# One kernel, one change: the recurrence's triangular inverse loads its operands at once, stores on GpSimd's queue, and its second half is issued behind the first half's recurrence

## The chip, the cores and the metric

The kernel runs on one core of a Trainium2 chip, in float32 with split products (each operand as a high and a low part, three matmuls per product). The metric is the device time in microseconds (us) of one execution. Engine names are those of the profile: PE (TensorE), DVE (VectorE), ACT (ScalarE), POOL (GpSimd), SP (SyncE, which issues nearly all DMAs).

## The reference, cut to what matters

Two blocks run one after the other on x of 1024 rows by 1024 columns. In the first, a projection feeds three mixers (an RWKV7 recurrence with 8 heads, a sparse attention with 4 heads, an attention to a memory), and their outputs, side by side, go through an out projection and a norm. The second block (a second mixer and a mixture of experts) is not touched by the change.

```python
def rwkv7_scan(r, decay, k, v, kk, a):
    def step(S, inp):
        r_t, w_t, k_t, v_t, kk_t, a_t = inp
        sa = einsum('bhvk,bhk->bhv', S, -kk_t)
        S = S * w_t + sa[..., None] * (kk_t * a_t) + v_t[..., None] * k_t
        return S, einsum('bhvk,bhk->bhv', S, r_t)
...
y = concat([rwkv7_group(...), nsa_group(...), memory_attention(...)])   # 512 + 256 + 256 columns
x = rms_norm(x + y @ w_out, norm_final_g)
```

The kernel does the recurrence in chunks. Inside a chunk the steps depend on each other through a lower triangular matrix, whose inverse is needed before the chunk's products.

## The kernel before

The first block's rows are cut into two halves of 512 rows, each of four tiles of 128 rows. A half goes through these steps, each a Python generator that issues instructions and yields a cost:

- `first_stage` and `att_proj`: the input projections. PE's products are pcm (L272); each weight piece is loaded (wraw, L229), copied by ACT to its high part (whi, L232) and subtracted by DVE to its low part (wlo, L233).
- `recur(H)`: first `inverse(H)`, then `rwkv_tile` for four tiles (masked products E on DVE, L757; pXk, L771; pX, L799), then the last tile's end.
- `attend(H)`: memory attention (`mem_tile`) and sparse attention (`nsa_tile`) for each tile. Both end in `finish_heads`, which norms the heads (DVE, with a power on POOL, L189), transposes them (PE's pfin, L898) and stores them to d_y.
- `third_stage(H)`: `close_first` with the out projection (`out_proj`), which reads d_y back (yr, L1147, with its parts yh and yl), multiplies (PE's pout, L1171), adds to the rows (DVE's rr, L1174) and norms them; then the second mixer. The out projection takes the column groups in the order 2, 3, 0, 1: group 2 is the sparse attention's, group 3 the memory attention's.

`inverse(H)` does, for the 64 blocks of 32x32 of each of two heads' halves at once: four times a load of two operands (AB, on SP's queue), a product (pN, L696), a mask (N on DVE, L698) and four stores of 32 KB to DRAM (d_n, L701); then one load of all of d_n into another layout (NTt, L704), and a forward substitution of 31 steps on DVE, each a product (scr, L712) and an addition (Ti, L714), one behind the other: 62 instructions, here called the chain. ACT makes a transposed copy (Tt, L716), and two stores (d_t) hand the result to `rwkv_tile`, which loads it as D and TT.

All four AB tiles use one buffer (tag "BK"), so that each load waits for the product before it.

What runs beside what is set by `weave`: each stream has a start time and a rate, the stream with the lowest time issues next, and each yielded cost times the rate moves it on. A scheduler then moves instructions within each engine's row, and each engine executes its row in order. There are three weaves. The second holds the projections, `recur(0)` and `attend(0)`; the third holds `third_stage(0)`, `recur(1)` and `attend(1)`, until the last two are through; the rest of `third_stage(0)` follows.

Of the kernel before, what the change touches and what calls it, by code (L numbers as in the profile page):

```python
# [25 lines left out]
CS = 64  # L26
# [74 lines left out]
def body(tc, a, out, stop=None, dbg=None):  # L101
    nc = tc.nc
# [89 lines left out]
    H2 = T // 2  # L192
# [16 lines left out]
    def R1(name):  # L209
        return ps_tile("r", name)  # L210
# [462 lines left out]
    d_n = dram.tile([2, 4, 8, 4, 32, 32], F32, name="d_n")  # L673
    d_t = dram.tile([2, 2, 4, 8, 4, 32, 32], F32, name="d_t")
# [6 lines left out]
    def rtile(tag, shape, bufs=1, name=None):  # L681
        return rw.tile([P] + shape, F32, tag=tag, name=name or tag, bufs=bufs)

    def inverse(H):

        ts = slice(TH * H, TH * H + TH)
        for p in range(4):
            AB = rtile("BK", [2, H2], name="AB")
            nc.sync.dma_start(ch(AB[:, 0]), d_AR[8 * H:8 * H + 8, :, p, 0].rearrange("c q t -> q c t"))
            nc.sync.dma_start(by_tile(AB[:, 1]), d_BK[ts, :, p, 0].rearrange("n q t -> q n t"))  # L690
            yield 0.6
            ps = R1("pN")
            for c in range(8):
                sl = slice(c * CS, (c + 1) * CS)
                for r in lohi:
                    nc.tensor.matmul(ps[r, sl], AB[r, 1, sl], AB[r, 0, sl], start=True, stop=True)  # L696
            N = rtile("UV", [8, CS], name="N")
            nc.vector.tensor_tensor(N, ch(ps), emask[:, None, 0:64].to_broadcast([P, 8, 64]), op=OP.mult)  # L698
            for q in range(4):
                b = (q % 2) * 32  # L700
                nc.sync.dma_start(d_n[H, q, :, p].rearrange("c s t -> s c t"), N[q * 32:q * 32 + 32, :, b:b + 32])  # L701
            yield 0.401
        NTt = rtile("X0", [32, 32], name="NTt")
        nc.sync.dma_start(NTt.rearrange("p s t -> p (s t)"), d_n[H].rearrange("q c p s t -> (q c p) (s t)"))  # L704
        Ti = rtile("GT", [32, 32], name="Ti")
        nc.gpsimd.memset(Ti, 0.0)
        nc.gpsimd.memset(Ti.rearrange("p a b -> p (a b)")[:, 0:1024:33], 1.0)
        scr = rtile("scr", [256])
        for s in range(31):
            nt, nj = 31 - s, s + 1  # L710
            sv = scr[:, :nt * nj].rearrange("p (t j) -> p t j", j=nj)
            nc.vector.tensor_tensor(sv, NTt[:, s, s + 1:32, None].to_broadcast([P, nt, nj]),  # L712
                                    Ti[:, s, None, 0:nj].to_broadcast([P, nt, nj]), op=OP.mult)
            nc.vector.tensor_tensor(Ti[:, s + 1:32, 0:nj], Ti[:, s + 1:32, 0:nj], sv, op=OP.add)  # L714
        Tt = rtile("X0", [32, 32], name="Tt")
        nc.scalar.activation(Tt, Ti.rearrange("p t j -> p j t"), AF.Copy)  # L716
        for x, src in ((0, Ti), (1, Tt)):
            nc.sync.dma_start(d_t[H, x].rearrange("q c p s t -> (q c p) (s t)"), src.rearrange("p a b -> p (a b)"))
        yield 0.979

    state = [None]
# [367 lines left out]
        yield 0.097  # L1089

    def recur(H):
        yield from inverse(H)
        for i in range(TH * H, TH * H + TH):
            yield from rwkv_tile(i)
        yield from ends.pop()

    def attend(H):
        for i in range(TH * H, TH * H + TH):
            yield from mem_tile(i)
            yield from nsa_tile(i)  # L1100
# [496 lines left out]
    def weave(*streams, until=()):  # L1597


        live = [[t0, n, g, rate] for n, (g, t0, rate) in enumerate(streams)]  # L1600
        wait = set(until) or set(range(len(streams)))
        while wait:
            s = min(live, key=lambda z: z[:2])
            c = next(s[2], None)
            if c is None:
                live.remove(s)
                wait.discard(s[1])
            else:
                s[0] += c * s[3]
# [11 lines left out]
    def narrow(g, J, V):  # L1621
        ring.update(J=J, V=V)
        yield from g

    def third_stage(H):
        with ExitStack() as st:
            rows = yield from close_first(H, pool("wkD", 1, stack=st))
            h2 = turn_rows(rows)
        yield 6
        yield from second_mixer(H, h2)  # L1630

    weave((first_stage(0), 0, 1))
    ring.update(J=["pj", "s"])
    weave((chain(att_proj(0), mem_kv(), first_stage(1), att_proj(1)), 0, 1),
          (recur(0), 0, 3.135),
          (narrow(attend(0), ["pj"], ["v"]), 90.8, 1.849))
    s1.close()
    g0 = third_stage(0)
    weave((g0, 0, 1), (recur(1), 9.9, 1.618), (attend(1), 0.1, 0.554), until=(1, 2))
    if "y" in dbg:  # L1640
        nc.sync.dma_start(dbg["y"], d_y)
    s2.close()
# [281 lines left out]
    with tc.manual_schedule(engines={mybir.EngineType.PE, mybir.EngineType.DVE, mybir.EngineType.Pool}):  # L1924
# [6 lines left out]
        with tc.For_i(0, n_ov, 1) as j:  # L1931
# [13 lines left out]
            b = NPAIR % 2  # L1945
# [68 lines left out]
```

## Time and profile before

| | |
|---|---|
| time, median of 3 runs | 2520.39 us (2517.54 to 2523.12) |
| the profiled execution | 2521.22 us, of which 2519.4 us are its span |
| PE busy | 2386.9 us, 95% of the span |
| DVE busy | 1543.9 us, 61% |
| ACT busy | 754.7 us, 30% |
| POOL busy | 349.6 us, 14% |
| granted TensorE clock, mean | 0.978 |

The span runs from the first to the last instruction of the execution. The granted clock is a share of full speed: 1.00 is the level of 2.4 GHz, 0.50 that of 1.2 GHz, and a value between is a window that held both. A matmul at 0.50 stays busy twice as long, so a window's time lost for PE is its length less busy time times clock.

### The profile page before, as it was taken

The page shows a single profiled execution, that of the slowest core. Times are in us where ns is not written, and L with a number is a line of the kernel's source. Part 1 is how long each engine was busy: PE and PEld are TensorE (multiplying, and loading weights), DVE is VectorE, ACT ScalarE, POOL GpSimd, SP SyncE. Part 2 cuts the span into 40 slices and gives each one's busy share as a digit, 9 for nine tenths or more (in the row PEclk, how much of TensorE's full clock was granted, in tenths as well). Part 3 has the DMA queues.
Part 4 walks back from the last instruction along what each step waited for, and adds up shares of the span by engine and source line. Part 5 has one row for each costly group of instructions (what it writes and reads, how often), then busy time and mean ns, then how long its engine had stood idle before and what let it go on. Part 6 is the DMA issues. An engine that isn't in the chain of part 4 may idle for free. (4 is left out here: it accounts for less than half of the span.)

```text
span 2519.4 us, 36225 instructions
## 1 busy us (share of the span) xinstructions
PE 2386.9 (95%) x13656; PEld 1545.4 (61%) x13656; DVE 1543.9 (61%) x3112; ACT 754.7 (30%) x1488; POOL 349.6 (14%) x472
## 2 busy tenths in 40 slices
PE   8989999999979999999999969999999999999997
PEld 6766777777757777787888824444444444444443
DVE  5537666754877676666665655555555555555555
ACT  4423554433445443343242411111111111111112
POOL 3000000010001011101120011111111111111112
PEclk9989999999979999999999979999999999999999
DMA  7667545544533222545355678999999999999991
GB/s 172 163 146 194 154 109 133 130 114 130 162 93 88 72 79 61 156 142 158 104 176 170 244 284 364 411 409 413 408 408 413 410 408 413 407 410 409 413 408 79
DMA packets 354176, 605.65 MB, mean 240 GB/s; under 512 B 124584, under 2 KB 299056, under 8 KB 329424
## 3 DMA queue, kind: packets, MB, share of 16 engines
q1 hardware_dynamic: 346592, 594.49, 65.6%
q0 software_dynamic: 5168, 8.69, 1.0%
q8 instruction: 109, 1.79, 0.3%
q14 instruction: 67, 0.55, 0.1%
q10 hardware_dynamic: 2240, 0.14, 0.1%
HBM read 563.46 MB, written 48.30 MB: 243 GB/s over the span
## 5 line engine op out<-in xcount | busy, mean ns | idle before, releaser
L1740 PE MATMUL pgu<-mw,xT 128*64 128x512 f32 x2048 | 461.4, 598 | 2.3 <-DVE up L1745 2.3
L272 PE MATMUL pcm<-hTh,whi 128*128 128x512 f32 (+1 forms) x912 | 369.2, 405 | 0.2 <-ACT whi L232 0.2
L272 PE MATMUL pcm<-hTh,wlo 128*128 128x512 f32 (+1 forms) x912 | 363.4, 398 | 0.5 <-DVE wlo L233 0.5
L272 PE MATMUL pcm<-hTl,whi 128*128 128x512 f32 (+1 forms) x912 | 363.6, 399 | 0.0
L233 DVE TENSOR_TENSOR wlo<-wraw,whi 128x512 fp32r<-128x512 f32 (+1 forms) x300 | 209.4, 702 | 185.9 <-ACT whi L232 160.7
L232 ACT ACTIVATE whi<-wraw 128x512 fp32r<-128x512 f32 (+1 forms) x300 | 187.0, 626 | 442.0 <-PE pcm L272 314.3
L1740 PEld LDWEIGHTS pgu<-mw,xT 128*64 128x64 f32 x2048 | 142.8, 137 | 265.9 <-issue 255.0
L1798 DVE TENSOR_TENSOR mw<-psp,mw 128x1024 f32<-128x1024 f32 x248 | 292.5, 1220 | 8.8 <-PE psp L1790 5.1
L1790 PE MATMUL psp<-yo,wt 128*128 128x512 f32 x1024 | 274.9, 410 | 4.1 <-DVE mw L1798 3.2
L1790 PEld LDWEIGHTS psp<-yo,wt 128*128 128x128 f32 x1024 | 182.7, 188 | 139.0 <-issue 80.6
L1768 PE MATMUL pyd<-mw,hT 128*64 128x512 f32 x1008 | 229.9, 598 | 2.3 <-DVEq L1931 2.3
L1744 DVE SCALAR_TENSOR_TENSOR mth<-mth,pgu 64x512 f32<-64x512 f32 x64 | 43.5, 679 | 290.5 <-ACT mth L1743 290.4
L272 PEld LDWEIGHTS pcm<-hTh,wlo 128*128 128x128 f32 (+1 forms) x912 | 170.7, 187 | 40.7 <-issue 3.8
L272 PEld LDWEIGHTS pcm<-hTh,whi 128*128 128x128 f32 (+1 forms) x912 | 170.8, 187 | 39.1 <-issue 5.4
L272 PEld LDWEIGHTS pcm<-hTl,whi 128*128 128x128 f32 (+1 forms) x912 | 171.0, 187 | 35.4 <-issue 2.9
L1743 ACT ACTIVATE mth<-pgu,rq 64x512 f32<-64x512 f32 x64 | 43.8, 684 | 493.4 <-PE pgu L1740 493.4
L1775 ACT ACTIVATE yo<-pyd,gt 64x512 fp32r<-64x512 f32 x128 | 87.6, 685 | 305.6 <-PE pyd L1768 304.3
L1777 DVE SCALAR_TENSOR_TENSOR yo<-pyd,gt,yo 64x512 fp32r<-64x512 f32 x128 | 96.0, 750 | 126.3 <-ACT yo L1775 125.3
L1783 POOL TENSOR_SCALAR wt<-rcon,tfs 128x128 fp32r<-128x128 f32 x256 | 150.4, 607 | 148.4 <-PE psp L1790 127.5
L1768 PEld LDWEIGHTS pyd<-mw,hT 128*64 128x64 f32 x1008 | 66.9, 136 | 126.7 <-issue 123.2
L1802 POOL DMA_INDIRECT xg<-d_x,idxt x32 | 34.4, 1076 | 690.0 <-issue 630.9
L1171 PE MATMUL pout<-whi,yh 128*128 128x512 f32 x256 | 107.4, 421 | 5.2 <-DVE rr L1174 5.1
(480 smaller groups left out, 3431.7 us busy)
## 6 DMA issues: line engine op xcount, KB each, us to landing
mw<-in_w_gate_dram SPq DMA_DIRECT2D x64, 2048.0 KB, 13.8
mw<-in_w_up_dram SPq DMA_DIRECT2D x64, 2048.0 KB, 9.5
mw<-in_w_down_dram SPq DMA_DIRECT2D x63, 2048.0 KB, 13.8
wraw<-in_w_in_dram SPq DMA_DIRECT2D x216, 256.0 KB, 3.1
wraw<-in_w_out_dram SPq DMA_DIRECT2D x32, 256.0 KB, 2.6
yr<-d_y SPq DMA_DIRECT2D x32, 256.0 KB, 3.1
d_x<-rr SPq DMA_DIRECT2D x16, 512.0 KB, 3.0
wraw<-in_w_o_dram SPq DMA_DIRECT2D x32, 256.0 KB, 3.0
```

The source lines that it names most:

```text
L232: nc.scalar.activation(hi, raw, AF.Copy)
L233: nc.vector.tensor_sub(lo, raw, hi.bitcast(F32))
L272: nc.tensor.matmul(ps[0:n], w, h[:, k], start=(k == 0 and j == 0), stop=(k == KD - 1 and j == 2))
L1171: nc.tensor.matmul(ps, y[:, t], w, start=(k == 0 and j == 0), stop=(k == 1 and j == 2))
L1740: nc.tensor.matmul(ph_[lohi[s]], xT[:, k], pieces[s][:, k * 512:(k + 1) * 512], start=(k == 0), stop=(k == KD - 1))
L1743: nc.scalar.activation(th, ph_[0:64], AF.Tanh, scale=rq[:, 0, h:h + 1])
L1768: nc.tensor.matmul(py[s][lohi[s]], hT[:, k, lohi[h]], piece[:, k * 1024 + s * 512:k * 1024 + s * 512 + 512], start=(k == 0), stop=(k == 3))
L1775: nc.scalar.activation(y[:, 0, 512 * s:512 * s + 512], py[s][o], AF.Copy, scale=gt[o, h:h + 1])
L1777: nc.vector.scalar_tensor_tensor(y[:, 1, 512 * s:512 * s + 512], py[s][o], gt[o, h:h + 1], y[:, 0, 512 * s:512 * s + 512].bitcast(F32), op ...
L1783: nc.gpsimd.tensor_scalar(w[0:n, i], iota[0:n], sh[0:n, i:i + 1], None, op0=OP.is_equal)
L1790: nc.tensor.matmul(ps[:, cs], w[0:n], yo[0:n, x, cs], start=(start and x == 0), stop=(x == 1))
L1798: nc.vector.tensor_tensor(x2, ps, x2, op=OP.add)
```

## The change

1. All eight loads of AB are issued together, into four buffers (three in a tile of tag "E", one of tag "BK"); the four N tiles get buffers of their own (tags "UV" and "GT").
2. The 16 d_n stores, the NTt load and the two d_t stores of each half are issued on GpSimd's queue, no longer on SP's.
3. `inverse(1)` is issued at the end of `recur(0)`, in the second weave, no longer at the start of `recur(1)`, in the third.
4. Rates: `attend(0)` in the second weave 1.849 to 1.76. In the third weave `recur(1)` starts at 0.2 with rate 1.9 (before 9.9 and 1.618), and `attend(1)` has rate 0.8 (before 0.554).

```diff
@@ -684,24 +684,26 @@
     def inverse(H):
 
         ts = slice(TH * H, TH * H + TH)
-        for p in range(4):
-            AB = rtile("BK", [2, H2], name="AB")
+        e_, b_ = rtile("E", [3, 2, H2], name="AB"), rtile("BK", [2, H2], name="AB")
+        ABs = [e_[:, 0], e_[:, 1], e_[:, 2], b_]
+        Ns = [t[:, p] for t in (rtile("UV", [2, 8, CS], name="N"), rtile("GT", [2, 8, CS], name="N")) for p in range(2)]
+        for p, AB in enumerate(ABs):
             nc.sync.dma_start(ch(AB[:, 0]), d_AR[8 * H:8 * H + 8, :, p, 0].rearrange("c q t -> q c t"))
             nc.sync.dma_start(by_tile(AB[:, 1]), d_BK[ts, :, p, 0].rearrange("n q t -> q n t"))
-            yield 0.6
+        yield 0.6
+        for p, (AB, N) in enumerate(zip(ABs, Ns)):
             ps = R1("pN")
             for c in range(8):
                 sl = slice(c * CS, (c + 1) * CS)
                 for r in lohi:
                     nc.tensor.matmul(ps[r, sl], AB[r, 1, sl], AB[r, 0, sl], start=True, stop=True)
-            N = rtile("UV", [8, CS], name="N")
             nc.vector.tensor_tensor(N, ch(ps), emask[:, None, 0:64].to_broadcast([P, 8, 64]), op=OP.mult)
             for q in range(4):
                 b = (q % 2) * 32
-                nc.sync.dma_start(d_n[H, q, :, p].rearrange("c s t -> s c t"), N[q * 32:q * 32 + 32, :, b:b + 32])
+                nc.gpsimd.dma_start(d_n[H, q, :, p].rearrange("c s t -> s c t"), N[q * 32:q * 32 + 32, :, b:b + 32])
             yield 0.401
         NTt = rtile("X0", [32, 32], name="NTt")
-        nc.sync.dma_start(NTt.rearrange("p s t -> p (s t)"), d_n[H].rearrange("q c p s t -> (q c p) (s t)"))
+        nc.gpsimd.dma_start(NTt.rearrange("p s t -> p (s t)"), d_n[H].rearrange("q c p s t -> (q c p) (s t)"))
         Ti = rtile("GT", [32, 32], name="Ti")
         nc.gpsimd.memset(Ti, 0.0)
         nc.gpsimd.memset(Ti.rearrange("p a b -> p (a b)")[:, 0:1024:33], 1.0)
@@ -715,7 +717,7 @@
         Tt = rtile("X0", [32, 32], name="Tt")
         nc.scalar.activation(Tt, Ti.rearrange("p t j -> p j t"), AF.Copy)
         for x, src in ((0, Ti), (1, Tt)):
-            nc.sync.dma_start(d_t[H, x].rearrange("q c p s t -> (q c p) (s t)"), src.rearrange("p a b -> p (a b)"))
+            nc.gpsimd.dma_start(d_t[H, x].rearrange("q c p s t -> (q c p) (s t)"), src.rearrange("p a b -> p (a b)"))
         yield 0.979
 
     state = [None]
@@ -1089,10 +1091,13 @@
         yield 0.097
 
     def recur(H):
-        yield from inverse(H)
+        if H == 0:
+            yield from inverse(0)
         for i in range(TH * H, TH * H + TH):
             yield from rwkv_tile(i)
         yield from ends.pop()
+        if H == 0:
+            yield from inverse(1)
 
     def attend(H):
         for i in range(TH * H, TH * H + TH):
@@ -1633,10 +1638,10 @@
     ring.update(J=["pj", "s"])
     weave((chain(att_proj(0), mem_kv(), first_stage(1), att_proj(1)), 0, 1),
           (recur(0), 0, 3.135),
-          (narrow(attend(0), ["pj"], ["v"]), 90.8, 1.849))
+          (narrow(attend(0), ["pj"], ["v"]), 90.8, 1.76))
     s1.close()
     g0 = third_stage(0)
-    weave((g0, 0, 1), (recur(1), 9.9, 1.618), (attend(1), 0.1, 0.554), until=(1, 2))
+    weave((g0, 0, 1), (recur(1), 0.2, 1.9), (attend(1), 0.1, 0.8), until=(1, 2))
     if "y" in dbg:
         nc.sync.dma_start(dbg["y"], d_y)
     s2.close()
```

Adding up the yielded costs, `attend(1)` now ends at 126.6 weave units and `recur(1)` at 130.0; before, they ended at 87.7 and 128.5. From the change on, lines after the inverse have numbers 2 higher, and from `attend` on 5 higher (pout is L1176, pfin L900, the chain L714 and L716).

**The first half on DVE.** These are consecutive places of DVE's row at the first inverse, before: the last three N products' masks (N), the gate's bias and copy (put, gl), the compression's sums (cin), and the chain's start (scr, Ti).

```order
L524 TENSOR_TENSOR late<-pcm,vec 128x512
L698 TENSOR_TENSOR N<-pN,cst 128x512
L608 TENSOR_SCALAR put<-pcm,vec 12x512
...
L614 COPY gl<-pgl 128x48
L698 TENSOR_TENSOR N<-pN,cst 128x512
...
L698 TENSOR_TENSOR N<-pN,cst 128x512
L233 TENSOR_TENSOR wlo<-wraw,whi 128x512
L581 TENSOR_TENSOR xc<-pd,xc 128x512
L757 TENSOR_TENSOR E<-pE,cst 128x6x64
L712 TENSOR_TENSOR scr<-NTt,Ti 128x31
```

And now, with the last N on top:

```order
L700 TENSOR_TENSOR N<-pN,cst 128x512
L522 TENSOR_TENSOR kcl<-pcm,vec 128x16
L524 TENSOR_TENSOR kcv<-pcm,vec 128x512
L524 TENSOR_TENSOR late<-pcm,vec 128x512
L759 TENSOR_TENSOR E<-pE,cst 128x6x64 x6
L714 TENSOR_TENSOR scr<-NTt,Ti 128x31
L716 TENSOR_TENSOR Ti<-Ti,scr 128x31
L714 TENSOR_TENSOR scr<-NTt,Ti 128x60
...
L608 TENSOR_SCALAR put<-pcm,vec 12x512
...
L614 COPY gl<-pgl 128x48
```

The fourth N stands ahead of the compression's operands (kcl, kcv, late), and the chain's first steps stand ahead of the gate's bias (put) and copy (gl), which they followed before.

**The second half on DVE.** This is DVE's row from the last N of the second inverse to the start of its chain, now in the second weave; before, N and chain stood among the out projection's additions (rr).

```order
L700 TENSOR_TENSOR N<-pN,cst 128x512
L540 TENSOR_TENSOR cin<-pcmp,cin 128x32
L543 SCALAR_TENSOR_TENSOR cth<-cth,cin 128x32
L544 TENSOR_SCALAR cact<-cth 128x32
L1072 TENSOR_TENSOR ob<-pob,ob 128x256
L1038 TENSOR_REDUCE mx<-pS 128x1
L1076 TENSOR_TENSOR ob<-ob,den 128x256
L1038 TENSOR_REDUCE mx<-pS 128x1
L1089 TENSOR_TENSOR on<-on,ob 128x256
L233 TENSOR_TENSOR wlo<-wraw,whi 128x512 x2
L555 COPY kcT_251<-pkc 64x63
L714 TENSOR_TENSOR scr<-NTt,Ti 128x31
```

Ten rows (eleven instructions) stand between the last mask and the chain, whose 62 steps then stand mixed with about 50 instructions of the projections and of the attention's end.

**The junction of the second and third weave on PE.** Before: attention's last pfin of the sparse heads, the memory attention's products (pM, pTm, pom), its pfin, and the out projection's first pout.

```order
L898 MATMUL pfin<-cst,on 128x128 x2
L925 MATMUL pM<-memk,qh 128x256
...
L941 MATMUL pTm<-cst,prm 128x128 x8
L948 MATMUL pom<-memv,pTm 128x64 x8
L898 MATMUL pfin<-cst,om 128x128 x2
L970 MATMUL pc<-kcT_251,qn 128x128 x2
L1171 MATMUL pout<-whi,yh 128x512
```

Now, with 17 pcm behind the pfin (in the place of the first mark), and with pE of the recurrence's next tile:

```order
L900 MATMUL pfin<-cst,on 128x128 x2
L272 MATMUL pcm<-hTl,whi 128x512
...
L927 MATMUL pM<-memk,ql 128x256
L757 MATMUL pE<-AR,BK 64x192 x8
L927 MATMUL pM<-memk,qh 128x256
...
L757 MATMUL pE<-AR,BK 64x192
L943 MATMUL pTm<-cst,prm 128x128 x4
L757 MATMUL pE<-AR,BK 64x192 x7
L950 MATMUL pom<-memv,pTm 128x64 x2
L1176 MATMUL pout<-whi,yh 128x512
```

Projection products and the next tile's pE stand between the pfin and the first pout.

## Rows read from the trace of the kernel before

**Rows 1.** Windows: length; busy PE, PEld, DVE, ACT, POOL; granted clock, DMA share, GB/s.

```profile
600.00:625.00 25.00, 19.84 (x124) 16.08 (x124) 12.81 (x27) 9.23 (x23) 1.01 (x1) 0.86 0.37 104
625.00:650.00 25.00, 20.88 (x97) 17.13 (x96) 16.87 (x37) 8.73 (x20) 1.01 (x1) 0.80 0.69 225
700.00:725.00 25.00, 17.42 (x74) 13.37 (x75) 22.33 (x64) 5.22 (x14) 2.66 (x2) 0.77 0.21 59
725.00:750.00 25.00, 17.79 (x81) 13.45 (x79) 18.91 (x50) 16.32 (x33) 2.65 (x4) 0.77 0.38 121
750.00:775.00 25.00, 22.66 (x207) 17.29 (x208) 16.22 (x41) 13.79 (x31) 2.53 (x5) 0.71 0.34 106
775.00:800.00 25.00, 24.09 (x209) 18.87 (x208) 16.57 (x42) 16.33 (x38) 1.65 (x1) 1.00 0.25 68
150.00:175.00 25.00, 19.09 (x215) 13.17 (x213) 9.07 (x19) 3.61 (x6) 0.00 (x0) 0.84 0.64 145
175.00:200.00 25.00, 21.87 (x168) 14.71 (x168) 12.03 (x32) 4.93 (x8) 2.49 (x2) 0.81 0.73 193
1000.00:1025.00 25.00, 23.44 (x168) 19.62 (x167) 13.07 (x30) 7.30 (x14) 4.10 (x3) 1.00 0.21 67
```

**Rows 2.** Timeline of PE at the second weave's end: start, length, instruction, idle before.

```profile
619.99 0.66 PE L898 MATMUL pfin<-cst,on 128*128 128x128 f32 x2 [4.37 <-DVE on L894]
633.33 0.77 PE L1171 MATMUL pout<-whi,yh 128*128 128x512 f32 x1
...
637.48 0.40 PE L1171 MATMUL pout<-wlo,yh 128*128 128x512 f32 x1
637.72 0.40 PE L1171 MATMUL pout<-whi,yl 128*128 128x512 f32 x1
```

**Rows 3.** Waits of PE from 700 to 730 us.

```profile
PE pout L1171 <- DVE rr L1174: 5.1, 2, 3.3
```

**Rows 4.** Groups of DVE's instructions from 684 to 742 us (the second inverse's chain).

```profile
L714 DVE TENSOR_TENSOR Ti<-Ti,scr 128x31 f32<-128x31 f32 (+15 forms) x31 | 10.4, 335 | 0.0
L712 DVE TENSOR_TENSOR scr<-NTt,Ti 128x31 f32<-128x31 f32 (+15 forms) x31 | 10.3, 334 | 0.0
L1174 DVE TENSOR_TENSOR rr<-pout,rr 128x512 f32<-128x512 f32 x13 | 8.9, 686 | 1.1 <-PE pout L1171 1.1
```

**Rows 5.** Windows ahead of the second weave's end, and of the second chain.

```profile
575.00:600.00 25.00, 24.90 (x146) 19.30 (x143) 10.89 (x27) 10.27 (x22) 0.00 (x0) 1.00 0.46 132
600.00:615.00 15.00, 15.00 (x93) 12.18 (x94) 7.05 (x14) 6.67 (x14) 0.00 (x0) 1.00 0.18 53
684.00:742.00 58.00, 46.98 (x283) 34.86 (x281) 52.03 (x150) 22.14 (x53) 3.90 (x4) 0.87 0.27 81
```

**Rows 6.** Timeline of PE, the first half's pN products.

```profile
141.55 1.15 PE L696 MATMUL pN<-AB 64*64 64x64 f32 x32
159.71 1.15 PE L696 MATMUL pN<-AB 64*64 64x64 f32 x32
175.58 1.97 PE L696 MATMUL pN<-AB 64*64 64x64 f32 x32 [3.32 <-DMA AB<-d_BK]
```

**Rows 7.** Timeline of SP and of DVE, the first half's NTt and chain start.

```profile
182.12 0.33 SPq L704 DMA_DIRECT2D NTt<-d_n  x1
190.34 0.18 DVE L712 TENSOR_TENSOR scr<-NTt,Ti 128x31 f32<-128x31 f32 x1
```

**Rows 8.** DMA issues, 0 to 1100 us: tile, queue, count, KB each, median us to landing.

```profile
d_n<-N SPq DMA_DIRECT2D x32, 32.0 KB, 2.3
vec<-in_rwkv_ln_w_dram POOLq DMA_DIRECT2D x1, 2.0 KB, 3.4
vec<-in_nsa_cmp_pos_dram POOLq DMA_DIRECT2D x2, 8.0 KB, 7.4
```

**Rows 9.** Groups of POOL's instructions, 0 to 1100 us: its DMA issues, shortest and longest.

```profile
L1133 POOL DMA_DIRECT2D vec<-in_router_e_b_dram x1 | 0.6, 567 | 0.0
L495 POOL DMA_DIRECT2D vec<-in_nsa_cmp_pos_dram x2 | 2.2, 1134 | 0.0
```

## The prediction

> **What bounds the kernel now.** PE is busy 95% of the span, so first the share and the windows of 25 us: where is PE not at work, or at work at half clock? A window's lost time is its length less busy time times granted clock. Undisturbed windows lose about 0.9 us (25 - 24.09) [rows 1]. Around the two inverses it is otherwise:
>
> - First half, 150 to 200 us: 25 - 19.09 x 0.84 = 9.0 and 25 - 21.87 x 0.81 = 7.3, together 16.3, which is 14.5 more than normal [rows 1].
> - Junction of the weaves, 600 to 650: 7.9 + 8.3 = 16.2, 14.4 more than normal [rows 1].
> - Second half, 700 to 775: 11.6 + 11.3 + 8.9 = 31.8, 29.1 more than normal [rows 1].
>
> Then the timeline and the waits, for the cause of each. At the junction the attention's last pfin is at 619.99 and the first pout at 633.33 [rows 2]: 13.3 us in which the head's norm, the store to d_y, the load of yr and its split follow each other, and PE has little but the memory attention's small products. From 700 to 730 PE waits 5.1 us for rr [rows 3], and DVE is why: in 684 to 742 it is busy 52.0 of 58 us [rows 5], of which the chain takes 10.4 + 10.3 = 20.7 [rows 4]. Without it DVE has 52.0 - 20.7 = 31.3 us of work there, beside PE's 46.98 x 0.87 = 40.9 us at full clock: PE would be the bound. In the first half PE waits for the fourth AB, 3.3 us, and reaches the fourth pN only at 175.58 [rows 6]; NTt is issued at 182.12, and the chain starts at 190.34 [rows 7].
>
> **The change, part by part.** All instructions stay; only places and queues change, so the sum is made of lost time. I count against the profiled execution, 2521.2 us; the median is 0.8 lower.
>
> *Taken away at the junction and behind it: 14.4 + 29.1 = 43.5 us.* That is the most that moving the second inverse can bring: its 20.7 us of DVE work leave the out projection, and work that was in the third weave (the next tile's pE and pXk) is ready at the junction. Five things come back.
>
> 1. *What is left at the junction: 4 us.* Behind the pfin PE now has 17 pcm, products of the size of pout, which follow each other by 0.24 us [rows 2], so 4.1 us, and 16 pE and the memory attention's products, which I estimate at as much again: 8 to 9 of the 13.3 us are covered. Bounds 0 and 7.
> 2. *NTt comes late: 3 us.* Where the last N is masked, four d_n have still to be issued, to land, then NTt likewise. The issue on POOL is 0.57 to 1.13 us [rows 9], I take 0.85; the landing from POOL 3.4 to 7.4 [rows 8], I take 4 for d_n, which has little data (2.3 from SP), and 5 for NTt. That is 4 x 0.85 + 4 + 0.85 + 5 = 13 us. Eleven instructions stand between the last mask and the chain on DVE, some 10 us as PE feeds them; behind the chain's first step all of DVE's row waits, wlo too, and PE runs dry a little later. Bounds 0 and 8.
> 3. *DVE is full ahead of the junction: 7 us.* From 575 to 615 DVE is busy 10.89 + 7.05 = 17.9 of 40 us and PE nearly all of it [rows 5]. With the chain's 20.7 it is 38.6 of 40, and some 4 us of masks (E, N) are moved there too: the stretch is 3 us too short, and a row this full cannot follow PE without gaps. I take 7; the bounds are 0 (the chain fills gaps alone) and 20.7 (it only moves).
> 4. *What is left of the out projection's losses: 6 us.* The half's closing norm keeps its chain of DVE, POOL and ACT, and the first tile of the second half now loads D and TT behind d_t on SP, whose landing from POOL can be 7.4 [rows 8], with weight loads queued behind. Bounds 2 and 12.
> 5. *The third weave's end: 3 us.* Attention now ends at 126.6 of 130 units, so its last pfin stands just ahead of the second half's out projection, with a chain like the 13.3 us of the junction [rows 2]; I count 8 to 10 of it covered by the recurrence. Before, the window at 1000 lost 1.6 us [rows 1]. Bounds 0 and 10.
>
> *The first half: 2 us gained.* With four buffers the fourth pN follows the pcm that the second one followed (159.71, [rows 6]); N4 is done at about 160.5, and 13 us later NTt is there, at about 174, against 190.3 [rows 7]. The chain starts 16 us earlier, but its first steps now stand ahead of the gate's bias and copy in DVE's row. DVE gets there at about 166, and then holds pgl and what follows on PE for 8 us, with some half clock behind it, as the windows at 150 and 175 show it now. So 11 to 13 us of the 14.5 are lost again in another way. Bounds -4 and +9.
>
> Moving 38 transfers off SP frees about a third of a microsecond of its row each (NTt's issue 0.33, [rows 7]), over two long stretches; PE's waits for loads there were those for AB, which are counted, so I add nothing. The rates of the third weave cost nothing by themselves: PE is the bound there, whatever stands in its row.
>
> Sum: 43.5 + 2 - (4 + 3 + 7 + 6 + 3) = 22.5. The profiled execution would take 2498.7 us, the median 2498.
>
> A rule speaks against the second part. What the rows show is that POOL's issues take 0.57 to 1.13 us [rows 9], in a stretch with little on DVE. The Trainium skill ("SBUF — State Buffer", section "SBUF: two separate sides") says that descriptors of a DMA on GpSimd's queue are written by GpSimd through a port pair that certain DVE instructions lock for their whole length, and that a DMA of about 620 ns took about 3100 ns beside a DVE copy. By its figures (estimate: 2.5 us more for each of 17 transfers) a half's NTt would be some 40 us later and the kernel slower than before; no row of before has POOL issue DMAs beside a busy DVE. It is rival B.
>
> **The rivals.**
>
> *A. The chain only moves.* DVE's full row ahead of the junction costs PE the whole 20.7 us [rows 4] in place of 7. For it: 38.6 of 40 us in the row. Against it: PE's rows there are long runs of pcm whose wlo can be made ahead. 22.5 - 13.7 = 8.8 less than before: 2511.6.
>
> *B. GpSimd's queue is slow (slower).* If an issue takes c us, the last d_n is out at the later of N4 + 4c and N1 + 16c. In the first half N1 is at 142.7 and N4 at 160.5; in the second I estimate them 10 us apart, from the fourteen rows between them on DVE. At c = 0.85 that is the forecast. If each issue also waits out one DVE instruction like rr (0.686, [rows 4]), c is 1.53, and NTt is later by 4 us in the first and 12 in the second half, 16 together. DVE executes in order, so PE stands for it, with some half clock: 1.2 us for each, 19 us, and 2517 remains, nearly no change. At c = 2.0 it is 12 + 19 = 31 us later, 37 us lost: 2535. It decides at c = 1.6. For it: d_n's pieces are small, 128 bytes by the code, and many, and no issue from POOL beside a busy DVE was seen. Against it: the longest issue of 1.13 [rows 9].
>
> *C. The end of the third weave stands open.* The whole 13.3 us [rows 2] come back at about 1000 to 1020, with half clock on the products behind them, in all 15 in place of 3: 2510. The row's window there was undisturbed before [rows 1].
>
> *D. All comes back but the norm.* Parts 1, 2, 3 and 5 are covered, and the first half gains 7: 43.5 + 7 - 6 = 44.5 less: 2476.
>
> **How the numbers follow.** Forecast (2488 to 2507) 0.50, A 0.16, B 0.14, C 0.07, D 0.10, and no effect at all 0.03. About 0.2%, 5 us, is what a measurement of this kernel can tell from no change (its three runs lie 5.6 us apart). Faster: 0.50 + 0.15 of A + 0.06 of C + 0.10 of D = 0.81, of which I take 0.03 off for sums of bad bounds: 0.78. Slower: 0.10 of B and 0.02 of those sums, 0.12. Same: the rest, 0.10. The range, 2478 to 2518, holds the forecast, A, C, nearly D and the mild end of B; the bounds of parts 3 and 4 alone reach 2518. The forecast's own range is 2488 to 2507.
>
> **What would show it.** Right: the windows at 700 to 775 lose under 12 us in place of 31.8, pout no longer waits for rr there, the chain stands ahead of the first pout, and DVE is busy over 85% in the 35 us ahead of it. The first half's NTt is issued at about 165 to 170, and PE still has a gap between 165 and 180, now ahead of pgl. POOL's d_n issues take about 0.85 us. Wrong: issues over 1.6 us, or the chain starting later than 20 us behind the last N (B); losses over 15 us in the 40 us ahead of the first pout (A); a gap of over 8 us ahead of the second half's first pout (C). It would also be wrong if the out projection waited for wraw behind a D that waits for d_t: then part 4 is too small.

## The result, and the profile after

The changed kernel takes 2491.11 us (median of 4 runs, 2488.46 to 2492.93) against 2521.72 us of the kernel before, run beside it: ratio 0.9883, 95% interval 0.987 to 0.9896. That is 30.6 us less, where 22.5 were forecast. The profiled execution took 2492.9 us, its span 2491.0.

Windows of 25 us of the changed kernel, columns as in the rows of before (length; busy PE, PEld, DVE, ACT, POOL; granted clock; DMA):

```profile
150.00:175.00 25.00, 20.97 (x172) 12.97 (x170) 11.48 (x26) 3.84 (x7) 5.74 (x10) 1.00 0.81 210
175.00:200.00 25.00, 22.93 (x183) 17.69 (x184) 22.03 (x48) 5.68 (x10) 5.39 (x4) 0.86 0.59 159
575.00:600.00 25.00, 25.00 (x176) 19.21 (x176) 14.31 (x40) 9.24 (x20) 6.91 (x13) 1.00 0.74 201
600.00:625.00 25.00, 23.13 (x134) 18.04 (x135) 23.47 (x61) 9.16 (x21) 1.74 (x1) 1.00 0.34 105
625.00:650.00 25.00, 24.04 (x200) 17.98 (x191) 21.49 (x57) 10.55 (x21) 2.42 (x3) 1.00 0.85 283
700.00:725.00 25.00, 24.35 (x157) 17.83 (x156) 19.18 (x48) 10.95 (x24) 3.96 (x3) 1.00 0.19 54
725.00:750.00 25.00, 21.03 (x199) 15.13 (x197) 21.51 (x50) 15.64 (x33) 3.42 (x5) 0.85 0.53 167
750.00:775.00 25.00, 23.95 (x178) 19.24 (x177) 17.36 (x42) 15.06 (x33) 1.65 (x3) 0.87 0.32 92
1000.00:1025.00 25.00, 25.00 (x123) 20.70 (x122) 18.26 (x38) 8.48 (x14) 1.39 (x1) 1.00 0.80 212
```

Where windows of before lost 7.9 and 8.3 us at the junction [rows 1], those of after lose 25 - 23.13 = 1.9 and 1.0. From 700 to 775 the loss is 0.7 + 7.1 + 4.2 = 11.9 in place of 31.8. The first half's two windows lose 4.0 + 5.3 = 9.3 in place of 16.3. DVE is busy 23.5 and 21.5 of 25 us ahead of and at the junction, and PE works on beside it.

The timeline of PE at the junction, from the attention's last pfin of the sparse heads to the first pout:

```profile
616.21 0.41 PE L900 MATMUL pfin<-cst,on 128*128 128x128 f32 x2 [0.71 <-DVE on L896]
...
625.91 0.48 PE L1176 MATMUL pout<-whi,yh 128*128 128x512 f32 x1
```

Before, 13.3 us lay between the two [rows 2], at a granted clock of 0.50 from 620 on. Now it is 9.7 us, in which PE waits for 1.1 us (for a mask E) and is else at work, on pcm and on the next tile's pE.

The chain of the second half, as groups on DVE in the stretch 590 to 638 (busy, mean ns, idle before), and its first and last product on DVE's timeline:

```profile
L714 DVE TENSOR_TENSOR scr<-NTt,Ti 128x31 f32<-128x31 f32 (+15 forms) x31 | 10.4, 335 | 0.6 <-DMA NTt<-d_n 0.3
L716 DVE TENSOR_TENSOR Ti<-Ti,scr 128x31 f32<-128x31 f32 (+15 forms) x31 | 10.4, 335 | 0.3
```

```profile
591.75 0.19 DVE L714 TENSOR_TENSOR scr<-NTt,Ti 128x31 f32<-128x31 f32 x1 [0.34 <-DMA NTt<-d_n]
...
635.10 0.18 DVE L714 TENSOR_TENSOR scr<-NTt,Ti 128x31 f32<-128x31 f32 x1
```

The window of these 48 us:

```profile
590.00:638.00 48.00, 46.13 (x266) 35.07 (x264) 43.10 (x118) 19.03 (x39) 2.34 (x2) 1.00 0.55 178
```

The work is what it was, 10.4 + 10.4 us, and it lies over 43 us, between other instructions; before, it lay over 50 (690.24 to 740.6). DVE is as full as it was around the chain before, 43.1 of 48 us and 52.0 of 58 [rows 5], 90% in both. But PE was busy 46.1 of 48 us at full clock, where it had been busy 47.0 of 58 at 0.87. DVE waited 0.34 us for NTt at the chain's start.

GpSimd's issues (groups of POOL's instructions, 100 to 700 us) and their landing (DMA issues: count, KB each, median us to landing):

```profile
L703 POOL DMA_DIRECT2D d_n<-N x32 | 18.7, 590 | 26.3 <-DVE N L700 22.2 <-DVE Y L879 2.5 <-DMA d_n<-N 1.3
L706 POOL DMA_DIRECT2D NTt<-d_n x2 | 1.2, 578 | 7.0 <-DMA d_n<-N 4.5 <-issue 2.5
```

```profile
d_n<-N POOLq DMA_DIRECT2D x32, 32.0 KB, 3.5
NTt<-d_n POOLq DMA_DIRECT2D x2, 512.0 KB, 5.4
d_t<-Ti POOLq DMA_DIRECT2D x2, 512.0 KB, 3.6
```

An issue takes 0.59 us, near the shortest of before [rows 9]; a d_n store lands in 3.5 us, where SP's took 2.3 [rows 8].

### The profile page after: what moved, and what is told of

It is laid out like the page before. It is cut to its first block, busy times and chain, and to the rows that moved or that the text cites. A ratio compares the mean times of both kernels' runs of the same rounds, so it can differ in the third digit from the quotient of the medians.

```text
span 2491.0 us, 36174 instructions
## 1 busy us (share of the span) xinstructions
PE 2388.6 (96%) x13656; PEld 1539.5 (62%) x13656; DVE 1546.2 (62%) x3112; ACT 751.7 (30%) x1488; POOL 372.8 (15%) x510
## 5 line engine op out<-in xcount | busy, mean ns | idle before, releaser
L1749 DVE SCALAR_TENSOR_TENSOR mth<-mth,pgu 64x512 f32<-64x512 f32 x64 | 43.5, 679 | 293.0 <-ACT mth L1748 293.0
L1179 DVE TENSOR_TENSOR rr<-pout,rr 128x512 f32<-128x512 f32 x128 | 87.6, 686 | 36.9 <-PE pout L1176 32.2
```

Of the source, the lines that this page charges most:

```text
L1179: nc.vector.tensor_tensor(rr[:, sl], ps, rr[:, sl], op=OP.add)
```

## How lost time is counted in the experiments

For each kernel I add, over windows of 25 us, length less PE's busy time times granted clock. Some stretches, in us (a normal window loses 0.9, so the stretches have 3.6, 2.7, 2.7 and 4.5 that mean nothing):

| kernel | 150 to 250 | 575 to 650 | 700 to 775 | 775 to 900 | ratio to before, 95% interval | us less |
|---|---|---|---|---|---|---|
| before | 19.4 | 16.3 | 31.8 | 4.8 | 1 | 0 |
| after | 10.7 | 2.8 | 11.9 | 1.6 | 0.9883 (0.987 to 0.9896) | 29 |
| rate_first | 18.5 | 8.4 | 20.9 | 8.3 | 0.9955 (0.9937 to 0.9972) | 11 |
| rate_third | 18.8 | 16.2 | 18.8 | 2.1 | 0.999 (0.998 to 1.0) | 3 |
| buf_queue | 13.1 | 15.0 | 12.5 | 3.8 | 0.9953 (0.9936 to 0.997) | 12 |
| move_only | 15.9 | 8.1 | 12.9 | 1.9 | 0.9917 (0.9901 to 0.9934) | 21 |
| no_queue | 18.1 | 3.6 | 8.3 | 2.0 | 0.9909 (0.9893 to 0.9926) | 23 |
| queue_first | 12.6 | 5.8 | 8.2 | 2.8 | 0.9893 (0.9876 to 0.991) | 27 |
| old_rates | 10.7 | 11.4 | 12.8 | 6.5 | 0.9944 (0.9926 to 0.9962) | 14 |
| after_old_first | 12.7 | 15.0 | 7.6 | 2.8 | 0.9902 (0.9883 to 0.992) | 25 |
| after_old_third | 9.5 | 5.2 | 11.8 | 8.2 | 0.9931 (0.9914 to 0.9947) | 17 |
| before_short_chain | 17.6 | 16.2 | 8.1 | 2.1 | 0.9921 (0.9903 to 0.9938) | 20 |
| after_short_chain | 10.0 | 2.5 | 8.5 | 2.5 | 0.9877 (0.9858 to 0.9896) | 31 |
| later_chain | 11.0 | 8.3 | 9.4 | 2.8 | 0.9875 (0.9858 to 0.9891) | 32 |

The last column is (1 - ratio) x 2520; the medians of the changed kernel and of the one before are 30.6 apart. An interval is about 4 us to each side, so kernels of the changed family that lie under 5 us apart are not told apart by their times. The stretches are of one execution, at fixed times, and a kernel that is ahead has other work in the same window; they point to a place and do not add up to the time. Up to 1250 us the sum of all stretches falls by 43 from before to after, while the first load of the experts' weights is issued 32.2 us earlier (1312.19 and 1279.99). Part of the difference is that some products keep PE busy longer than before, the pE above all (43.6 us in all before, 48.0 after); the rest is not explained.

## Experiments

My theory was that the place of the second inverse carries the gain: out of the out projection, under the projections. The rivals were that buffers and queue carry it, that the weaves' numbers do, and, from the prediction, that the chain only moves its cost (A) or GpSimd's queue is slow (B).

**The change taken apart.** `buf_queue` keeps the buffers and the queue and undoes the move and the rates:

```diff
     def recur(H):
-        if H == 0:
-            yield from inverse(0)
+        yield from inverse(H)
         for i in range(TH * H, TH * H + TH):
             yield from rwkv_tile(i)
         yield from ends.pop()
-        if H == 0:
-            yield from inverse(1)
...
-          (narrow(attend(0), ["pj"], ["v"]), 90.8, 1.76))
+          (narrow(attend(0), ["pj"], ["v"]), 90.8, 1.849))
...
-    weave((g0, 0, 1), (recur(1), 0.2, 1.9), (attend(1), 0.1, 0.8), until=(1, 2))
+    weave((g0, 0, 1), (recur(1), 9.9, 1.618), (attend(1), 0.1, 0.554), until=(1, 2))
```

> The changed kernel with the second inverse back at the start of the third weave and the old rates; four buffers and GpSimd's queue stay. Theory (place): only the first half's gain is left, with the 250 to 300 us stretch's loss against it: 2512 to 2518, and the windows at 600 to 650 and 700 to 775 lose 40 us or more again. Rival (buffers and queue carry it): 2495 to 2505.

12 us less than before, more than the theory gave and less than the rival. The junction keeps its loss, as expected. What I had not expected is the out projection. Windows of this kernel:

```profile
625.00:650.00 25.00, 21.49 (x98) 16.11 (x98) 17.20 (x37) 9.80 (x19) 3.35 (x5) 0.81 0.73 229
675.00:700.00 25.00, 20.93 (x146) 15.32 (x144) 22.93 (x59) 11.09 (x28) 0.00 (x0) 1.00 0.27 79
700.00:725.00 25.00, 20.44 (x87) 15.96 (x88) 19.38 (x56) 9.12 (x18) 3.21 (x4) 0.80 0.45 129
725.00:750.00 25.00, 24.69 (x258) 18.83 (x257) 19.65 (x44) 13.93 (x32) 2.45 (x3) 1.00 0.52 152
```

The chain still stands among the out projection's additions, but its operands are loaded at once and its N masks come within 4 us (611.6 to 614.8 on DVE, before 615.7 to 678.5), so that the chain starts at 650.8 in place of 690.2 and is spread over 59 us. The windows from 675 to 725 lose 4.1 + 8.6 us, as much as before (0.6 + 11.6); but those from 725 to 775, where the norm stands, lose 3.9 in place of 20.2 [rows 1]. So part of the out projection's 29 us came from the lateness of the chain, which ran on to 740 and into the norm, and not from its place. Whether the buffers or the queue brought this was not tried apart here.

`move_only` is the kernel before with the move and the new rates, one AB buffer and SP's queue. `no_queue` is the changed kernel with SP's queue; this is its edit:

```diff
-                nc.gpsimd.dma_start(d_n[H, q, :, p].rearrange("c s t -> s c t"), N[q * 32:q * 32 + 32, :, b:b + 32])
+                nc.sync.dma_start(d_n[H, q, :, p].rearrange("c s t -> s c t"), N[q * 32:q * 32 + 32, :, b:b + 32])
...
-        nc.gpsimd.dma_start(NTt.rearrange("p s t -> p (s t)"), d_n[H].rearrange("q c p s t -> (q c p) (s t)"))
+        nc.sync.dma_start(NTt.rearrange("p s t -> p (s t)"), d_n[H].rearrange("q c p s t -> (q c p) (s t)"))
...
-            nc.gpsimd.dma_start(d_t[H, x].rearrange("q c p s t -> (q c p) (s t)"), src.rearrange("p a b -> p (a b)"))
+            nc.sync.dma_start(d_t[H, x].rearrange("q c p s t -> (q c p) (s t)"), src.rearrange("p a b -> p (a b)"))
```

> The kernel before with the second inverse moved behind the first half's recurrence and the new rates; one AB buffer and SP's queue stay. Theory (the place of the second inverse carries the gain): the junction and the out projection keep what they won, the first half loses its 5 to 8 us again and the second half's single buffer costs 2 to 5 us: 2498 to 2505. Rival (buffers and queue carry it, the move is only possible because of them): the chain comes late and DVE stands before the junction: 2510 to 2525.

> The changed kernel with d_n, NTt and d_t on SP's queue again. Theory (place): the queue matters little, SP's transfers land sooner (2.3 against 3.5 us) but stand among the weight loads: 2490 to 2497. Rival (the queue is needed for the move): SP's row holds wraw behind the waits for N and Ti, PE waits for wraw: 2503 to 2520.

21 and 23 us less: both as the theory had it. Move and rates without buffers and queue bring two thirds of the gain. The queue is worth 6.6 us by the ratios (0.9909 and 0.9883), with an uncertainty of about 5; that it costs much, as rival B has it, is excluded. The buffers' 2 us between these two kernels are not told from zero. In `no_queue` SP needs 8.3 us for the first half's 16 d_n in one piece, and the half clock lasts longer there. Windows of 5 us of `no_queue`, then of the changed kernel:

```profile
165.00:170.00 5.00, 3.16 (x49) 2.16 (x51) 1.55 (x4) 0.63 (x1) 0.00 (x0) 0.92 1.07 258
170.00:175.00 5.00, 3.97 (x34) 2.33 (x30) 3.06 (x12) 0.00 (x0) 0.00 (x0) 0.50 0.58 133
175.00:180.00 5.00, 5.00 (x58) 3.93 (x54) 3.69 (x10) 2.25 (x4) 0.00 (x0) 0.50 0.78 205
180.00:185.00 5.00, 4.72 (x80) 4.10 (x76) 4.09 (x15) 0.28 (x1) 0.00 (x0) 0.50 0.02 3
185.00:190.00 5.00, 4.62 (x12) 3.41 (x12) 4.76 (x13) 0.11 (x1) 0.00 (x0) 0.53 0.60 130
```

```profile
170.00:175.00 5.00, 1.73 (x31) 1.16 (x29) 1.87 (x8) 0.00 (x0) 0.00 (x0) 1.00 0.34 112
175.00:180.00 5.00, 3.26 (x57) 3.05 (x57) 4.49 (x14) 2.19 (x4) 0.00 (x0) 0.61 0.01 1
180.00:185.00 5.00, 5.00 (x17) 4.05 (x17) 4.05 (x11) 0.63 (x1) 0.00 (x0) 0.71 0.75 210
185.00:190.00 5.00, 4.82 (x49) 3.38 (x47) 3.74 (x7) 1.11 (x2) 1.93 (x2) 1.00 0.78 216
```

With SP's queue PE stood for 1.8 us from 165 to 170, and is then at the level of 1.2 GHz for nearly the whole of 170 to 190, at work for 18.3 of the 20 us; with GpSimd's it stood for about 5 us of them, and was back at 2.4 GHz from 185. Counted as above, that is a loss of 10.7 us in the one and of 7.9 in the other, though PE is idle less in the first.

`queue_first` has GpSimd's queue for the first half alone:

```diff
-                nc.gpsimd.dma_start(d_n[H, q, :, p].rearrange("c s t -> s c t"), N[q * 32:q * 32 + 32, :, b:b + 32])
+                (nc.sync if H else nc.gpsimd).dma_start(d_n[H, q, :, p].rearrange("c s t -> s c t"), N[q * 32:q * 32 + 32, :, b:b + 32])
```

(and so for NTt and d_t).

> The changed kernel with GpSimd's queue for the first half's d_n, NTt and d_t, and SP's for the second half's. Theory (the queue's 5 us are won in the first half, where the stretch from 150 to 250 us lost 18.1 with SP's queue and 10.7 with GpSimd's): 2488 to 2491. Rival (they are won at the second weave's end, where SP also has the attention's stores and the out projection's loads): 2493 to 2497.

2493.96 us at ratio 0.9893, between `no_queue` and the changed kernel. The median lies in the rival's range, but the interval of the ratio is 2490 to 2498 us and reaches into the theory's. The stretch from 150 to 250 did fall from 18.1 to 12.6, as the theory said, but in which half the queue's few us are won stays open by the time.

**The rates.** The prediction gave them no price. `old_rates` is the changed kernel with all of the old numbers, `after_old_first` with the old first one (1.849), `after_old_third` with the old ones of the third weave, `rate_first` and `rate_third` the kernel before with only one or the other of the new:

```diff
-          (narrow(attend(0), ["pj"], ["v"]), 90.8, 1.849))
+          (narrow(attend(0), ["pj"], ["v"]), 90.8, 1.76))
```

(`rate_first`; the others by the same two lines of the change.)

> The changed kernel with the four old rates and the old start. Theory (place): the second weave is nearly the same, and in the third attention again ends early while the recurrence has nothing to wait for; DVE's load in the out projection's stretch rises with attention's: 2493 to 2502. Rival (the rates carry the gain of the third weave): 2505 to 2515.

> The kernel before with one number changed: the attention of the first half runs at rate 1.76 in the second weave, not 1.849, so that projection products stand behind its last pfin. Theory (the junction is a matter of cover, and the rate gives the cover): the stretch from 575 to 650 us loses 4 to 8 in place of 16, the out projection's 31.8 stays: 2507 to 2512. Rival (the junction is only filled because the second inverse's recurrence is ready there): 2515 to 2521.

> The changed kernel with rate 1.849 for the first half's attention and the new numbers of the third weave. Theory (cover at the junction): 575 to 650 loses 10 to 12 us as with all old rates, the rest is as changed: 2497 to 2502. Rival (the third weave's numbers made the difference of 12 to 15 us that all old rates cost): 2489 to 2493.

> The changed kernel with rate 1.76 for the first half's attention, but the old three numbers of the third weave. Theory (cover at the junction is what the rates give): 2490 to 2495. Rival (the third weave's numbers carry it): 2500 to 2505.

> The kernel before with the three new numbers of the third weave alone; the second inverse stays at the start of the second half's recurrence, which now starts at once and goes on more slowly. Theory (these numbers only fit the moved inverse): the chain comes a little earlier and the recurrence later, 2515 to 2523. Rival (spreading the attention is worth something by itself): 2505 to 2513.

`old_rates` is only 14 us faster than before, between theory and rival: half of the gain hangs on the numbers. That was my largest error. `rate_first`, one number, is 11 us faster by itself, as its theory had it. Its windows at the junction and in the out projection:

```profile
600.00:625.00 25.00, 22.49 (x144) 18.38 (x142) 13.83 (x28) 11.09 (x25) 1.01 (x1) 1.00 0.50 138
625.00:650.00 25.00, 22.29 (x123) 17.65 (x124) 18.42 (x41) 8.84 (x21) 1.01 (x1) 0.86 0.60 205
700.00:725.00 25.00, 17.04 (x85) 12.68 (x85) 22.90 (x71) 8.42 (x21) 2.60 (x2) 0.93 0.20 58
725.00:750.00 25.00, 20.25 (x165) 14.78 (x165) 17.59 (x35) 19.52 (x39) 4.61 (x7) 0.66 0.53 180
```

The loss from 575 to 650 falls from 16.3 to 8.4: with attention ending earlier than the projections, pcm stand behind its last pfin without any move of the inverse. In `old_rates` the inverse is moved, but the stretch still loses 11.4. Its windows there, and the wait of PE that is longest:

```profile
600.00:625.00 25.00, 20.02 (x117) 15.32 (x116) 22.37 (x65) 8.00 (x20) 1.04 (x1) 0.93 0.43 136
625.00:650.00 25.00, 21.54 (x168) 16.43 (x169) 16.44 (x38) 10.22 (x19) 2.17 (x3) 0.93 0.67 211
```

```profile
PE pE L757 <- DVE E L759: 3.7, 1, 3.7
```

There attention's tail, the chain and the next tile's masks meet on DVE, busy 22.4 of 25 us, and PE waits 3.7 us for a mask E. With the old first number alone (`after_old_first`) the same stretch loses 15.0, more than the 10 to 12 of its theory. By its time, 25 us less than before and between theory and rival, it is not told apart from the changed kernel; 700 to 775 loses 4.3 less there. So the first number sets the junction's loss, and how much of that remains in the time is not settled: 11 us without the rest of the change, 5 with it, the latter not told from zero.

The old numbers of the third weave (`after_old_third`) cost 12 us, against my theory, which had given 0 to 5, and in the rival's range. Most of what its trace shows of this is in 775 to 900, 8.2 in place of 1.6; the profiled executions of the two kernels lie 6.3 us apart. The wait of PE that is longest there:

```profile
PE pfin L900 <- DVE on L896: 4.3, 2, 3.5
```

With the new numbers the same pfin waits 0.2 us in that stretch. By themselves (`rate_third`) these numbers brought 3 us, at the edge of what the runs tell: the chain's stretch lost 18.8 in place of 31.8, but 900 to 1050 lost 9.3 in place of 4.2. With the moved inverse they bring 12, without it at most a few.

No run has all the new numbers without the move. Had apart, the first brings 11 and the other three 3 us; with the move `move_only` brings 21. By that the move is worth some 7 us there, an estimate from three ratios that is uncertain by as much; on top of buffers, queue and the old numbers it was worth 2. That the place of the second inverse alone carries the gain, my theory, is not shown.

**What the chain costs.** Two kernels leave the last 30 of the second half's 31 steps out (60 instructions of DVE, and with them that part of the inverse), once where the chain stood, once where it stands now:

```diff
-        for s in range(31):
+        for s in range(1 if H else 31):
```

> The kernel before, with the second half's forward substitution cut to its first step (2 of 62 instructions; 60 and their part of the inverse are left out). It shows what the chain costs where it stood. Theory (it costs the out projection's stretch nearly what DVE works on it): 2498 to 2504, 16 to 22 us less, the norm's losses stay. Rival (the stretch is held up by more than the chain, the late operands and the norm): 2506 to 2512.

> The changed kernel with the same 60 instructions left out of the second half. It shows what the chain costs where it now stands. Theory after the trace of the change (it lies in DVE's gaps, 43 us long, and costs nothing): 2488 to 2492. Rival (the forecast's term, 7 us of gaps on PE ahead of the junction, and more behind it): 2480 to 2485.

Where it stood the chain cost 20 us (interval 16 to 24), about all that DVE works on it, 20.7 [rows 4]. Windows of `before_short_chain`:

```profile
700.00:725.00 25.00, 23.95 (x225) 18.45 (x225) 20.06 (x48) 7.82 (x21) 2.02 (x2) 1.00 0.47 133
725.00:750.00 25.00, 22.93 (x196) 16.97 (x194) 18.40 (x38) 19.87 (x43) 3.87 (x7) 1.00 0.35 114
750.00:775.00 25.00, 23.32 (x146) 17.62 (x147) 20.14 (x50) 16.64 (x37) 2.65 (x2) 0.86 0.26 87
```

They lose 1.1 + 2.1 + 4.9 = 8.1 in place of 31.8 [rows 1]; what remains is the norm's part. Where it stands now, leaving the chain out brings 1.5 us by the ratios, with an uncertainty of about 6: nothing that the runs can tell from zero. Windows of `after_short_chain` ahead of the junction:

```profile
575.00:600.00 25.00, 24.99 (x177) 19.21 (x176) 11.08 (x25) 11.71 (x21) 6.99 (x13) 1.00 0.84 233
600.00:625.00 25.00, 23.67 (x146) 18.53 (x144) 15.04 (x32) 11.43 (x27) 1.04 (x1) 1.00 0.47 138
625.00:650.00 25.00, 23.80 (x187) 17.26 (x186) 19.21 (x42) 8.46 (x17) 1.01 (x1) 1.00 0.71 239
```

PE is as busy as with the chain, DVE is busy 11 to 19 us in place of 14 to 23.5: DVE had room for the chain, and PE did not wait for it. That decides against rival A, which had it cost 20.7 us here. The move can save less than these 20 us where the operands are early already: in `buf_queue` the out projection's stretch loses 12.5 in place of 31.8 before anything is moved.

**The wait at the chain's start.** In the first half, POOL issues the last d_n and then NTt; DVE's first step of the chain; and the longest wait of PE from 150 to 250:

```profile
160.07 2.30 POOL L703 DMA_DIRECT2D d_n<-N  x4 [7.31 <-DVE N L700]
...
166.89 0.58 POOL L706 DMA_DIRECT2D NTt<-d_n  x1 [4.52 <-DMA d_n<-N]
```

```profile
172.72 0.19 DVE L714 TENSOR_TENSOR scr<-NTt,Ti 128x31 f32<-128x31 f32 x1 [4.57 <-DMA NTt<-d_n]
```

```profile
PE pXk L771 <- DVE E L759: 5.0, 1, 5.0
```

DVE waits 4.57 us for NTt, and E and pXk behind it hold PE for 5.0. `later_chain` puts the chain a little later:

```diff
+        yield 1.5
         scr = rtile("scr", [256])
         for s in range(31):
```

> The changed kernel with a yield of 1.5 units between the load of NTt and the chain, in both halves; in the first, two of the masks E then stand behind the chain's first steps, and four ahead. Theory (DVE's 4.6 us wait for NTt at the chain's first step is what holds PE 5.0 us at pXk): where the chain is put a little later, 2486 to 2490, and the wait on DVE is under 3 us. Rival (the chain's length sets the time of the first tile, the wait only moves): 2489 to 2495.

In its trace DVE still waits 3.58 us for NTt, PE now 3.7 us for pgl in place of 5.0 for pXk, and 150 to 250 loses 11.0, as much as before the edit: in this execution the wait only moved. It is the slowest of the five runs, 2498 us, and tells little of the other four, which took 2485 to 2487. The ratio, 0.9875, is the lowest of all and the median is in the theory's range, but its interval holds the changed kernel's, and DVE's wait did not fall under 3 us as the theory wanted; that the edit makes the kernel faster is not shown.

## Why the prediction was right, and where it was not

The direction, the places and the rough size were right; the sum was 8 us short, and one step was wrong in kind. That the time came out near the forecast is in part luck: half of the gain hangs on numbers of the weaves, to which the sum gave nothing.

- **Taken away, 43.5 us.** The two places were right. The chain's price was right, 20.7 us of DVE work and 20 (16 to 24) by `before_short_chain`. Wrong is what the step credited: it gave all of it to the moved inverse. Half of the junction's part is brought by the first rate without any move (575 to 650 loses 8.4 in place of 16.3 in `rate_first`), and without that rate it stays (15.0 in `after_old_first`). Of the out projection's part the buffers and the queue bring much without a move (`buf_queue`). The parts overlap: 11 for the first rate and 12 for buffers and queue are had apart, and the move with the old rates on top of buffers and queue adds 2, not told from zero (`old_rates` against `buf_queue`).
- **"The rates of the third weave cost nothing by themselves: PE is the bound there."** This step failed: not in that the new numbers cost nothing, but in that the sum gave them no price either way. With the old ones the changed kernel is 12 us slower (`after_old_third`), and the second weave's rate, which the step does not name, brings 11 us by itself. PE is the bound on the mean, but the order decides how often its head waits, here 4.3 us for the head norm ahead of pfin. I had looked at what the rates do at the weave's end only.
- **Part 1, what is left at the junction: 4, and part 3, DVE full ahead of it: 7.** Mis-sized: the stretch 575 to 650 loses 2.8 in all, a normal loss. DVE is busy 23.5 of 25 us, as forecast, and PE does not mind: its longest wait there is 1.1 us for a mask E. `after_short_chain` measured part 3 by itself: 1.5 us by the time, which alone would not exclude 7, and in the stretch 2.5 in place of 2.8. The error was to price how full DVE's row is. It was as full around the chain before, and there PE waited 5.1 us for rr [rows 3]; here it has long runs of pcm whose wlo come in time.
- **Part 2, NTt late in the second half: 3.** It was 0.34. The sum of issue and landing was right: the last N was masked at 580.83, NTt was issued at 586.63, and the chain began at 591.75, 10.9 us after the mask, where NTt was forecast 13 us after it; the instructions between took as long.
- **Part 4, what is left of the out projection: 6.** It was 11.9 - 2.7 = 9.2. PE waited 1.0 us for D behind d_t, of which I had feared more; most of it is the norm's stretch at 735 to 750 with the half clock behind it.
- **Part 5, the third weave's end: 3.** 900 to 1050 loses 6.3 in place of 4.2, 2 us.
- **The first half: 2 gained.** 19.4 - 10.7 = 8.7 gained from 150 to 250, 3.6 lost again from 250 to 300 (10.7 in place of 7.1): 5. The mechanism is nearly as told: the chain starts at 172.7 (forecast 174), DVE's row waits for NTt, and PE stands, but 5.0 us and not 8, and ahead of pXk and not of pgl.
- **Not in the sum:** the experts' start gives some back. Their first product is 33.4 us earlier than before (1475.18 and 1441.75), the last of their pyd products 28.9 us (2486.12 and 2457.22). The windows behind the first product, before and after:

```profile
1475.00:1500.00 25.00, 19.94 (x76) 6.45 (x75) 6.51 (x21) 1.36 (x2) 4.38 (x6) 0.87 0.73 283
1500.00:1525.00 25.00, 23.46 (x123) 8.08 (x123) 22.14 (x90) 4.01 (x6) 0.00 (x0) 1.00 0.97 392
```

```profile
1442.00:1467.00 25.00, 19.94 (x73) 6.15 (x72) 6.01 (x18) 1.36 (x2) 4.36 (x6) 0.84 0.70 275
1467.00:1492.00 25.00, 23.90 (x104) 7.81 (x104) 21.01 (x86) 4.00 (x6) 0.00 (x0) 0.88 0.92 364
```

PE is busy about as long, but the clock was 0.84 and 0.88 where it had been 0.87 and 1.00. Counted as above the two windows lose 7.7 + 1.5 us before and 8.2 + 4.0 after, 3.0 more. Why the clock stayed low longer was not tried.

The parts by these sizes, with 1.0 us left of the junction's 14.4: 43.5 + 5 - (1.0 + 9.2 + 2 + 3.0) = 33, against 30.6 measured. The sizes are of one execution each.

Of the signs named ahead, four came as told: 700 to 775 loses 11.9, just under 12; pout waits 0.5 us for rr there; the first half's NTt is issued at 166.89; and from 591 to 626 DVE is busy 32.1 of 35 us, 92%. The chain does not stand ahead of the first pout: it ends 10 us behind it, at 635.8. POOL's issues took 0.59 us, not 0.85.

Rival A is excluded by `after_short_chain`; B by the 32 issues of d_n, 0.58 to 0.71 us each, and by `no_queue`, which is slower and not faster. The prediction said that no issue from POOL beside a busy DVE had been seen. That was a misreading: where POOL issued its loads before, at 0.57 to 1.13 us [rows 9], DVE was busy 10.5 of 11.9 us. The windows of these issues, and of twelve d_n issues of the changed kernel:

```profile
14.25:26.10 11.85, 11.85 (x55) 9.88 (x56) 10.54 (x26) 7.05 (x16) 11.85 (x16) 1.00 0.92 102
570.86:577.90 7.04, 6.84 (x84) 5.64 (x85) 4.10 (x11) 0.63 (x1) 7.04 (x12) 1.00 0.70 196
```

Beside these twelve DVE was busy 4.1 of 7.0 us, and an issue took 0.59 us. The rule of the Trainium skill ("SBUF — State Buffer", section "SBUF: two separate sides"), by which GpSimd cannot write descriptors while DVE runs certain instructions, such as a copy of float32 within SBUF, is not put to the test by this: beside the d_n issues DVE ran mostly products and sums of two operands, and no copy. Rival C did not come: 0.9 us of wait for the last pfin. D was nearly reached in parts 1 to 3 and in the first half (5 us of 7), not in parts 4 and 5.

## What to carry to other kernels

A long chain of short dependent instructions cost about its whole length in one place (20 us) and nothing that could be told from zero in another, with DVE 90% busy around it in both. So do not look only at how full the chain's engine is, but at what the bounding engine waits for in the same row: here PE needed the additions rr at once in the one, and in the other had products whose operands were ready. That this is the whole difference was not tried by a run. When a change moves a step and also touches the numbers by which streams are woven, price the numbers as an edit of their own: here one rate brought 11 us without the rest, and the move without the rates brought 2. And operands that come one by one through a single buffer can hold a chain back far: with four buffers and the other queue the chain started 39 us earlier in the same place (`buf_queue`).

## What was not expected of the hardware

- Half clock can cost more than the idle time ahead of it. With SP's queue PE stood for 1.8 us from 165 to 170 and for 1.7 from 170 to 190, less than with GpSimd's, but stayed at 1.2 GHz for nearly all of the latter: 9.0 of the 10.7 us lost there are clock. With GpSimd's queue 7.9 were lost, 5.2 of them idle.
- 32 stores of 32 KB, in pieces of 128 bytes, were issued from GpSimd at 0.59 us each, near the shortest of the loads that it issued before (0.567), and landed in 3.5 us where SP's landed in 2.3; the loads of 512 KB landed in 5.4.
